# Four merge tiles moved to seven products, their sums prepared beside the second branch

## The chip, the cores and the metric

The kernel runs on one core of a Trainium2 chip. Its engines are named as in the profile: PE (TensorE, the matrix engine; PEld are its weight loads), DVE (VectorE), ACT (ScalarE), POOL (GpSimd), and SP (SyncE), which here only issues DMAs. Each engine works through its own instructions in order. The metric is the device time of one launch in microseconds.

## The reference

One layer of an encoder with three parallel branches, for a prompt of 512 rows and a sample of 256 rows, each with 16 meta rows in front. The model width is 2048, everything is fp32.

```
h = rmsnorm(z, norm_g)
cols = h @ w_in                     # to u_a, gate_a, q, k, v, gate_b, glr, x_c, gate_c, merge
y_a = s5_mixer(u_a, ...)  * silu(gate_a)      # state space model; GLU at its end: z * sigmoid(z @ w_glu + b)
y_b = gla_mixer(q, k, v, glr, ...) * silu(gate_b)   # gated linear attention, chunks of 64
y_c = rglru_mixer(x_c, ...) * silu(gate_c)    # convolution and gated linear recurrence
gates = sigmoid(merge).reshape(b, l, 3, 2048)
m = gates_0 * (y_a @ w_out_a) + gates_1 * (y_b @ w_out_b) + gates_2 * (y_c @ w_out_c)
out = rmsnorm(z + m @ w_o)          # the meta rows are dropped
```

The part of `w_in` that matters here is `merge`: 3 x 2048 columns, in the kernel 48 tiles of 128 columns.

## The kernel before

Everything is kept transposed: 128 model columns on the partitions, the rows of both sequences beside one another as 784 columns (16 meta, 512 prompt, 256 sample). The normalised x is held on chip in 16 tiles of 128, each split in two halves `xh` and `xl` (`split`: a ScalarE copy to fp32r and a VectorE subtraction), and written to memory as `xnorm`. An fp32 product is three matmuls: high by high, high by low, low by high.

A tile of `w_in` of 128 columns is projected in one of two ways. The first is the plain one: 16 k tiles x 3 x 2 halves of 384 columns = 96 matmuls (`proj`, L199, or `fill_step`, L273, one k at a time: a step is 6 matmuls). A tile takes two weight loads of 512 KB, each split in halves `hi` and `lo`. The second is Strassen's (`strassen`, `products`, L1149): two tiles together, with the 16 k tiles in two halves and the 768 columns in two halves, need seven products in place of eight, each over 8 k tiles, in four quarters `sb` of 42 matmuls: 168 for two tiles in place of 192. It needs sums of x: three of 384 columns for each k (operands 0, 1, 2), and a fourth that overwrites the second half of x itself (`t2`). `NG2` pairs are gates and `NST` pairs are merge tiles.

The program runs the branches one after another: S5, GLA, LRU, then the Strassen stage, then the output projections. Merge tiles done the plain way are no stage of their own: their steps are put between the instructions of the branches, to keep PE at work while it would wait. How many is set by a count of VectorE's work: `tick` emits a step for each 1/rate us of it, with the rate of the stage from `FILLS` (`pace`). In S5 the stages are the scan, the chunk_out steps (L652 to L655, eight of them, one after another through a round trip `kt` to `kd` to `tp` in memory on ScalarE's queue) and the end: the gelu of y (tiles `fu`, `fy`, `ft`, giving z0 to z3 as `fz`, with halves `fh` and `fl`) and then the GLU with `w_glu` (`fw`, L728, 96 matmuls). `flush` ends an open tile, and what is left of the merge tiles stands at the end of LRU as `cover`, beside which the x sums of the Strassen stage are made (`sums`, and for the overwritten part `last_sum`, after the cover). A scheduler then sets the order on each engine by its own estimate, so that the order in the code is not the one in the program.

SP issues nearly all loads in order; a load waits until its target tile is free, and what is behind it waits too.

Of the kernel before, what the change touches and what calls it, by code (L numbers as in the profile page):

```python
# [6 lines left out]
F32 = mybir.dt.float32  # L7
F32R = mybir.dt.float32r
I32 = mybir.dt.int32
AF = mybir.ActivationFunctionType  # L10
ALU = mybir.AluOpType
# [5 lines left out]
NT = NP_ + NS  # L17
# [3 lines left out]
HN = NT // 2  # L21
MAGIC = 12582912.0
FILLS = (0.2, 0.7, 1.6, 0.8, 1.1, 0, 0, 0)
# [3 lines left out]
NST = 15  # L27
# [4 lines left out]
XS = 2  # L32
# [63 lines left out]
def build(tc, A, out_p, out_s):  # L96
# [12 lines left out]
    xnorm = drm.tile([16, 128, NT], F32, name="xnorm")  # L109

# [628 lines left out]
def branch_gla(E):  # L739
    tc, A = E["tc"], E["A"]  # L740
    V, S, PE, SP = E["V"], E["S"], E["PE"], E["SP"]
    col, split, proj, evac, tick, psB = (E[k] for k in ("col", "split", "proj", "evac", "tick", "psB"))
# [11 lines left out]
    def tmp():  # L754
        return lp.tile([128, T], F32, name="tmp", bufs=4)

# [25 lines left out]
    for hp in range(2):  # L782
# [139 lines left out]
        for h in range(2):  # L922
# [22 lines left out]
            tick()  # L945
    lp.release()
# [613 lines left out]
def strassen(E):  # L1560
# [11 lines left out]
    sh, sl = [[None] * 8 for i in range(3)], [[None] * 8 for i in range(3)]  # L1572
    for k in range(8):
        for i in range(3):
            sh[i][k] = sp.tile([128, HN], F32R, name=f"sh{i}{k}")
            sl[i][k] = sp.tile([128, HN], F32R, name=f"sl{i}{k}")
    xp = tc.alloc_tile_pool(name="stx", bufs=1, reuse_waits="tile")

    def load(k, o, n, **kw):
        x = xp.tile([128, n], F32, **kw)  # L1580
        (S if k % 8 < XS else SP).dma_start(x[:], xnorm[k, :, o:o + n])
        return x[:]

    def sums(k):
        xa = load(k, 0, NT, name="xa", bufs=2)
        s_, x, u = load(k + 8, HN, HN, name="x", bufs=2), xa[:, :HN], xa[:, HN:]
        V.tensor_tensor(out=s_, in0=s_, in1=u, op=add)
        split(sh[0][k][:], sl[0][k][:], s_)
        V.tensor_tensor(out=s_, in0=s_, in1=x, op=sub)
        split(sh[1][k][:], sl[1][k][:], s_)  # L1590
        V.tensor_tensor(out=u, in0=u, in1=x, op=sub)
        split(sh[2][k][:], sl[2][k][:], u)

    def last_sum(k):

        x = load(k + 8, 0, HN, name="x", bufs=2)
        s_ = xp.tile([128, HN], F32, name="y", bufs=2)[:]
        V.tensor_tensor(out=s_, in0=sh[1][k][:].bitcast(F32), in1=sl[1][k][:].bitcast(F32), op=add)
        V.tensor_tensor(out=s_, in0=x, in1=s_, op=sub)
        split(xh[k][:, t2], xl[k][:, t2], s_)  # L1600

    n = max(1, len(merges))
    for k in range(8):
        sums(k)
        while len(merges) > max(1, n * (7 - k) // 8):
            E["cover"](16)
    E["cover"](16 * len(merges) + 16)

    xp.release()
    tp = tc.alloc_tile_pool(name="stt", bufs=1, reuse_waits="tile")  # L1610
    xp = tc.alloc_tile_pool(name="sty", bufs=2, reuse_waits="tile")
# [14 lines left out]
    def operand(a, k):  # L1626
        if isinstance(a, int):
            return sh[a][k][:], sl[a][k][:]
        tk, ts = k + 8 * (a[1] == "2"), t1 if a[0] == "1" else t2
        return xh[tk][:, ts], xl[tk][:, ts]  # L1630

    ahead = []
    for sb in range(4):
        if sb < 3:
            ahead.append(weights(0, sb))
        last_sum(2 * sb)
        last_sum(2 * sb + 1)
    xp.release()
# [28 lines left out]
    free = [f"s{p}{i}{k}" for k in range(8) for i in range(3) for p in "hl"]  # L1667
    yh, yl = [], []
    for k in range(8):
        h = E["act"].tile([128, NT], F32R, name=f"h{8 + k}")  # L1670
        l = E["act"].tile([128, NT], F32R, name=f"l{8 + k}")
        for o in (0, HN):
            yr = sp.tile([128, HN], F32, name=free.pop(0))
            SP.dma_start(yr[:], E["yspill"][k, :, o:o + HN])
            split(h[:, o:o + HN], l[:, o:o + HN], yr[:])
        yh.append(h)
        yl.append(l)
# [118 lines left out]
```

## Time and profile before

| | |
|---|---|
| time, median of 3 runs | 2037.04 us (2035.94 to 2038.36) |
| profiled execution, its own time | 2038.42 us |
| its span, first to last instruction | 2036.6 us |
| PE busy | 2003.8 us, 98% |
| DVE busy | 1504.9 us, 74% |
| ACT busy | 808.2 us, 40% |
| DMA | 252.12 MB, mean 124 GB/s |

The times of the rows below are of the profiled execution, counted from the start of its span. An instruction's length in the matmul rows overlaps with its neighbours; the distance of starts tells what one costs. In the profile S5's chunk_out steps lie at 286 to 350 us, its GLU ends at 412, the last cover begins at 766 and the first Strassen product stands behind it.

### The profile page before, as it was taken

To read this page: it belongs to the slowest core of one execution; us is meant where nothing else is said; L and a number is where in the kernel's file an instruction comes from. 1 tells how busy PE (TensorE), PEld (TensorE's weight loads), DVE (VectorE), ACT (ScalarE), POOL (GpSimd) and SP (SyncE) were. 2 spreads that over 40 slices of the span, in tenths; PEclk is the share of its full clock that TensorE was granted. 3 is DMA by queue.
4 is the path that set the end of the run, shared out by engine and by line. 5 is a ranking of instruction groups with operands and counts; after the bars stand their busy time and mean duration, and the time that the engine had idled before them with its cause. 6 is when DMAs were issued, how large, how long until landed. Compare 5 with 4: busy or idle time off the path is not lost.

```text
span 2036.6 us, 30982 instructions
## 1 busy us (share of the span) xinstructions
PE 2003.8 (98%) x12228; PEld 1972.5 (97%) x12228; DVE 1504.9 (74%) x2784; ACT 808.2 (40%) x1172; POOL 0.2 (0%) x4
## 2 busy tenths in 40 slices
PE   8999999999999999999999999999999999999997
PEld 8999999999989999999999999999999999999997
DVE  8988983656567876977676656665669989887778
ACT  7332111443437675433333222222235435533345
POOL 0000000000000000000000000000000000000000
PEclk9999999999999999999999999999999999999999
DMA  8762234421111323543443222322355335532256
GB/s 292 251 123 94 75 102 120 147 80 49 61 52 45 102 72 122 179 133 102 139 135 112 94 94 100 103 91 100 104 183 215 125 114 180 176 117 94 94 163 218
DMA packets 105378, 252.12 MB, mean 124 GB/s; under 512 B 18960, under 2 KB 39952, under 8 KB 105232
## 3 DMA queue, kind: packets, MB, share of 16 engines
q1 hardware_dynamic: 77072, 200.61, 30.8%
q10 hardware_dynamic: 28160, 49.53, 6.9%
q8 instruction: 96, 1.57, 0.3%
q14 instruction: 50, 0.41, 0.1%
HBM read 200.65 MB, written 49.45 MB: 123 GB/s over the span
## 4 chain that ended last, share of the span: by engine, by line
PE 78%; DVE 13%; ACT 4%; DMA 3%; issue 1%; ACTq 0%; SPq 0%; DVEq 0%
PE pm L1149 24%; PE br L1149 23%; PE pm L199 10%; PE pm L273 5%; PE br L1422 4%; PE pm L1292 2%; PE br L1292 2%; DVE sc L61 2%; DVE W L61 2%; PE pm L332 2%; DVE lo L61 2%; ACT gt L89 1%; DMA c<-gspill 1%; DVE hb L61 1%; PE br L199 1%
## 5 line engine op out<-in xcount | busy, mean ns | idle before, releaser
L89 ACT ACTIVATE hi<-raw 128x768 fp32r<-128x768 f32 (+2 forms) x234 | 216.1, 924 | 482.8 <-PE br L1149 129.0
L61 DVE TENSOR_TENSOR lo<-raw,hi 128x768 fp32r<-128x768 f32 (+2 forms) x234 | 246.3, 1053 | 131.5 <-ACT hi L89 131.1
L61 DVE TENSOR_TENSOR lo<-t,hi 128x1024 fp32r<-128x1024 f32 x140 | 171.5, 1225 | 193.4 <-ACT hi L89 193.2
L89 ACT ACTIVATE hi<-t 128x1024 fp32r<-128x1024 f32 x140 | 148.4, 1060 | 279.6 <-PE pm L1149 138.3
L1149 PE MATMUL pm<-l,hi 128*128 128x384 f32 (+1 forms) x616 | 197.3, 320 | 0.0
L1149 PE MATMUL pm<-h,hi 128*128 128x384 f32 (+1 forms) x616 | 196.6, 319 | 0.2 <-ACT g L89 0.2
L1149 PE MATMUL pm<-h,lo 128*128 128x384 f32 (+1 forms) x616 | 196.6, 319 | 0.0
L1149 PE MATMUL br<-l,hi 128*128 128x384 f32 (+1 forms) x504 | 167.1, 331 | 0.0
L1149 PE MATMUL br<-h,hi 128*128 128x384 f32 (+1 forms) x504 | 165.9, 329 | 0.0
L1149 PE MATMUL br<-h,lo 128*128 128x384 f32 (+1 forms) x504 | 165.8, 329 | 0.0
L199 PE MATMUL pm<-h,hi 128*128 128x392 f32 (+1 forms) x608 | 161.8, 344 | 1.2 <-ACT xp L1022 1.2
L199 PE MATMUL pm<-h,lo 128*128 128x392 f32 (+1 forms) x608 | 159.5, 342 | 1.0 <-DVE lo L61 1.0
L199 PE MATMUL pm<-l,hi 128*128 128x392 f32 (+1 forms) x608 | 159.6, 341 | 0.0
L273 PE MATMUL pm<-h,lo 128*128 128x384 f32 x512 | 131.6, 338 | 2.5 <-DVE lo L61 2.5
L273 PE MATMUL pm<-h,hi 128*128 128x384 f32 x512 | 133.8, 342 | 0.0
L273 PE MATMUL pm<-l,hi 128*128 128x384 f32 x512 | 132.6, 340 | 0.0
L1149 PEld LDWEIGHTS pm<-h,hi 128*128 128x128 f32 x616 | 115.7, 188 | 0.7 <-ACT g L89 0.5
L1149 PEld LDWEIGHTS pm<-h,lo 128*128 128x128 f32 x616 | 116.0, 188 | 0.0
L1149 PEld LDWEIGHTS pm<-l,hi 128*128 128x128 f32 x616 | 115.7, 188 | 0.0
L199 PEld LDWEIGHTS pm<-h,hi 128*128 128x128 f32 x608 | 111.0, 188 | 2.7 <-ACT xp L1022 1.5
L199 PEld LDWEIGHTS pm<-h,lo 128*128 128x128 f32 x608 | 111.2, 188 | 1.5 <-DVE lo L61 1.3
L199 PEld LDWEIGHTS pm<-l,hi 128*128 128x128 f32 x608 | 110.6, 188 | 0.2
(358 smaller groups left out, 4799.6 us busy)
## 6 DMA issues: line engine op xcount, KB each, us to landing
raw<-in_w_st SPq DMA_DIRECT2D x92, 512.0 KB
raw<-in_w_in SPq DMA_DIRECT2D x74, 512.0 KB
gspill<-g ACTq DMA_DIRECT2D x48, 384.0 KB
raw<-in_w_ost SPq DMA_DIRECT2D x32, 512.0 KB
xr<-in_xT SPq DMA_DIRECT2D x31, 392.0 KB
m<-gspill SPq DMA_DIRECT2D x26, 384.0 KB
raw<-in_w_out SPq DMA_DIRECT2D x16, 512.0 KB
raw<-in_w_outc SPq DMA_DIRECT2D x16, 512.0 KB
```

The source lines that it names most:

```text
L61: return f(*a, **k)
L89: ins = self.eng.activation(**k)
L199: PE.matmul(ps[h][:, :nw], w[:, k, :], xx[kt][:, n0 + h * nw:n0 + (h + 1) * nw], start=(kt == 0 and j == 0), stop=(kt == 15 and j == 2))
L273: PE.matmul(ps[h][:, :HN], w[:, k % 8, :], xx[k][:, NM + h * HN:NM + (h + 1) * HN], start=(k == 0 and j == 0), stop=(k == 15 and j == 2))
L332: PE.matmul(ps0[2 * t + h][:, :HT], w[:, k, :], xx[kt][:, h * HT:(h + 1) * HT], start=(kt == 0 and j == 0), stop=(kt == 15 and j == 2))
L1149: PE.matmul(ps[j][:, :nt], w[:, wi, kk, :], x, start=(k == 0 and q == 0), stop=(k == n - 1 and q == 2))
L1292: PE.matmul(ps[h][:, :HN], w[:, 4 * b + k, :], yy[4 * b + k][:, h * HN:(h + 1) * HN], start=(k == 0 and j == 0), stop=(k == 3 and j == 2))
L1422: PE.matmul(po[:, :NS], x[:, n, :], y[k][:, ss], start=(first and j == 0), stop=(last and j == 2))
```

## The change

`NST` goes from 15 to 17, so that four more merge tiles (two pairs) are done by seven products and four fewer by plain steps. The rates of two S5 stages go down, of the chunk_out stage from 0.8 to 0.15 and of the gelu stage from 1.1 to 0.85. The sums of x are made by `strassen_sums` in GLA, one k at every third `tick` of it, on VectorE and ScalarE, and their halves are written to a new memory tensor `sspill`; the Strassen stage only loads them (`fetch`, `fetch_last`). The loads of the first two sums, which stood on ScalarE's queue (`XS`), are gone. At the end of the Strassen stage `yspill` is loaded in whole tiles of 768 columns.

```diff
-FILLS = (0.2, 0.7, 1.6, 0.8, 1.1, 0, 0, 0)
+FILLS = (0.2, 0.7, 1.6, 0.15, 0.85, 0, 0, 0)
-NST = 15
+NST = 17
-XS = 2
+    sspill = drm.tile([8, 2, 2, 128, NT], F32, name="sspill")
...
 def branch_gla(E):
+    def strassen_sums(k):
+        a, b = (lp.tile([128, NT], F32, name=n) for n in ("pa", "pb"))
+        SP.dma_start(a[:], E["xnorm"][k])
+        SP.dma_start(b[:], E["xnorm"][k + 8])
+        t1, t2 = slice(0, HN), slice(HN, NT)
+        TT = lambda o, x, y, op: V.tensor_tensor(out=o, in0=x, in1=y, op=op)
+        TT(b[:, t2], b[:, t2], a[:, t2], ALU.add)
+        TT(a[:, t2], a[:, t2], a[:, t1], ALU.subtract)
+        TT(a[:, t1], b[:, t2], a[:, t1], ALU.subtract)
+        TT(b[:, t1], b[:, t1], a[:, t1], ALU.subtract)
+        for i, x in enumerate((a, b)):
+            h = lp.tile([128, NT], F32R, name="ph")
+            S.activation(out=h[:], in_=x[:], func=AF.Copy)
+            TT(x[:].bitcast(F32R), x[:], h[:].bitcast(F32), ALU.subtract)
+            SP.dma_start(E["sspill"][k, i, 0], h[:].bitcast(F32))
+            SP.dma_start(E["sspill"][k, i, 1], x[:])
+    beside = [k for k in range(8)]
+    ticks = [0]
+    def tick():
+        E["tick"]()
+        ticks[0] += 1
+        if ticks[0] % 3 == 0 and beside:
+            strassen_sums(beside.pop(0))
...
 def strassen(E):
+    s1, s23, spill = {}, {}, E["sspill"]
+    def fetch(k):
+        s1[k] = [sp.tile([128, HN], F32R, name=f"s1{p}{k}") for p in "hl"]
+        s23[k] = [sp.tile([128, 2, HN], F32R, name=f"s2{p}{k}") for p in "hl"]
+        for p in range(2):
+            SP.dma_start(s1[k][p][:].bitcast(F32), spill[k, 1, p, :, HN:])
+            SP.dma_start(s23[k][p][:].bitcast(F32), spill[k, 0, p].rearrange("q (i n) -> q i n", i=2))
+    def fetch_last(k):
+        for p, x in enumerate((xh, xl)):
+            SP.dma_start(x[k][:, t2].bitcast(F32), spill[k, 1, p, :, :HN])
     for k in range(8):
-        sums(k)
-        while len(merges) > max(1, n * (7 - k) // 8):
-            E["cover"](16)
+        fetch(k)
     E["cover"](16 * len(merges) + 16)
...
     for sb in range(4):
         if sb < 3:
             ahead.append(weights(0, sb))
-        last_sum(2 * sb)
-        last_sum(2 * sb + 1)
+        fetch_last(2 * sb)
+        fetch_last(2 * sb + 1)
...
-        for o in (0, HN):
-            yr = sp.tile([128, HN], F32, name=free.pop(0))
-            SP.dma_start(yr[:], E["yspill"][k, :, o:o + HN])
-            split(h[:, o:o + HN], l[:, o:o + HN], yr[:])
+        yr = sp.tile([128, NT], F32, name=f"s2{'hl'[k % 2]}{k // 2}")
+        SP.dma_start(yr[:], E["yspill"][k])
+        split(h[:], l[:], yr[:])
```

The functions `sums`, `last_sum` and `load` go. Most lines of the changed file move (L793 is L821 there, L1149 is L1178, L1615 is L1623).

PE at the GLU of S5, before: the L728 matmuls of z0 (`fh_3583`), of z1 (`fh_3635`) and z2 (`fh_3675`) have projection matmuls (L199) between them.

```order
L728 MATMUL br<-fh_3583,fwl 128x384
L199 MATMUL pm<-h_102,hi 128x384 x2
L199 MATMUL pm<-l_103,hi 128x384 x2
L728 MATMUL br<-fh_3635,fwh 128x384 x4
L199 MATMUL pm<-h_102,lo 128x384 x2
L199 MATMUL pm<-h_123,hi 128x384 x2
L728 MATMUL br<-fl_3636,fwh 128x384
...
L199 MATMUL pm<-l_227,hi 128x384 x2
L199 MATMUL pm<-h_226,lo 128x384 x2
L199 MATMUL pm<-h_247,hi 128x384
L728 MATMUL br<-fh_3675,fwh 128x384 x4
```

The same place in the changed program: the L728 matmuls follow one another, here the end of z1 (`fh_3486`), z2 (`fh_3520`) and the first of z3 (`fh_3566`).

```order
L728 MATMUL br<-fl_3487,fwh 128x384
L728 MATMUL br<-fh_3486,fwl 128x384
L728 MATMUL br<-fh_3520,fwh 128x384 x4
L728 MATMUL br<-fl_3521,fwh 128x384
L728 MATMUL br<-fh_3520,fwl 128x384
...
L728 MATMUL br<-fh_3566,fwh 128x384 x3
...
L728 MATMUL br<-fl_3567,fwh 128x384
L728 MATMUL br<-fh_3566,fwl 128x384
```

In the changed program 144 projection matmuls (L199) stand ahead of this run of 96 and 10 behind it, then the gate matmuls of GLA (L821). Before, 84 merge and 96 projection matmuls stood ahead, 56 between, and 51 behind.

SP at the start of the Strassen stage, before: loads of `xnorm` (`xa`, `x`) for the sums, with the weights of the products (`in_w_st`) between them.

```order
L1581 DMA xa_7714<-xnorm_70 128x768
L1581 DMA x_7716<-xnorm_70 128x384
L1581 DMA xa_7727<-xnorm_70 128x768
L1581 DMA x_7729<-xnorm_70 128x384
L1615 DMA raw_7971<-in_w_st 128x1024
L1581 DMA xa_7740<-xnorm_70 128x768
L1581 DMA x_7742<-xnorm_70 128x384
L1581 DMA xa_7753<-xnorm_70 128x768
L1581 DMA x_7755<-xnorm_70 128x384
L1615 DMA raw_7999<-in_w_st 128x1024
L1581 DMA xa_7766<-xnorm_70 128x768
```

The same place in the changed program: the first two weight loads, then ten loads over the second half of x (`h_`, `l_` with a number, L1614), and behind these the loads of the sums (`s1h`, `s2h` and so on).

```order
L1623 DMA raw<-in_w_st 128x1024 x2
L1614 DMA l_104<-sspill 128x384
L1614 DMA h_103<-sspill 128x384
L1614 DMA l_125<-sspill 128x384
L1614 DMA h_124<-sspill 128x384
L1614 DMA l_165<-sspill 128x384
...
L1614 DMA h_206<-sspill 128x384
L1614 DMA l_207<-sspill 128x384
L1608 DMA s1h_7440<-sspill 128x384
L1609 DMA s2h_7442<-sspill 128x768
L1608 DMA s1l_7441<-sspill 128x384
```

The 32 loads of sums stand there in one row; the third weight load of the products follows the last of them, then the six last loads over x. Both the ten and the six write into tiles that the last plain merge tile reads.

## Rows read from the trace of the kernel before

**Rows 1.** The page, section 1: busy us, share of the span, instructions.

```profile
PE 2003.8 (98%) x12228; PEld 1972.5 (97%) x12228; DVE 1504.9 (74%) x2784; ACT 808.2 (40%) x1172; POOL 0.2 (0%) x4
```

**Rows 2.** Waits of PE: line <- releaser: us in total, times, longest us.

```profile
PE pm L273 <- DVE lo L61: 2.5, 2, 2.0
```

**Rows 3.** Windows: us, busy us (instructions) by engine, PEclk, DMA share, GB/s.

```profile
10.00:20.00 10.00, 9.74 (x53) 9.30 (x53) 9.81 (x11) 9.91 (x13) 0.00 (x0) 1.00 1.03 409
...
382.00:412.00 30.00, 27.87 (x155) 26.51 (x154) 20.71 (x21) 13.76 (x20) 0.00 (x0) 1.00 0.42 132
...
560.00:611.00 51.00, 49.42 (x280) 45.21 (x279) 34.63 (x79) 18.06 (x32) 0.00 (x0) 1.00 0.16 52
...
269.60:273.10 3.50, 3.50 (x13) 3.50 (x12) 3.31 (x16) 0.95 (x1) 0.00 (x0) 0.51 0.41 150
...
761.10:764.60 3.50, 3.50 (x12) 3.47 (x12) 0.00 (x1) 2.38 (x4) 0.00 (x0) 0.51 0.00 0
```

**Rows 4.** Chain of waits, 300 to 432 us: start us, us, what.

```profile
304.77 4.23 PE pm L273 x24
...
328.16 14.73 PE pm L273 x84
...
350.32 14.57 PE pm L273 x83
...
367.74 7.94 DMA fy<-yd
...
379.70 3.52 DMA fy<-yd
...
412.00 8.96 PE pm L199 x51
```

**Rows 5.** Timeline of ACT beside chunk_out: start us, us, instruction.

```profile
299.93 2.47 ACTq L644 DMA_DIRECT2D tp<-kd  x4
...
307.20 2.47 ACTq L644 DMA_DIRECT2D tp<-kd  x4
```

**Rows 6.** Timeline of ACT, 350 to 415 us (in brackets: idle before).

```profile
364.92 0.87 ACT L89 ACTIVATE g<-pm 128x384 f32<-128x384 f32 x2 [14.08 <-PE pm L273]
...
383.16 0.83 ACT L89 ACTIVATE fh<-fz 128x768 fp32r<-128x768 f32 x1
...
393.08 0.84 ACT L89 ACTIVATE fh<-fz 128x768 fp32r<-128x768 f32 x1 [0.69 <-DVE fz L61]
...
396.42 0.85 ACT L89 ACTIVATE fh<-fz 128x768 fp32r<-128x768 f32 x1 [1.02 <-DVE fz L61]
```

**Rows 7.** Chain of waits, 760 to 872 us.

```profile
766.48 16.98 PE pm L273 x97
...
850.38 2.11 PE br L1149 x12
```

**Rows 8.** Timeline of PE: the first instruction behind three idles.

```profile
268.94 0.62 PE L273 MATMUL pm<-h,lo 128*128 128x384 f32 x2 [2.04 <-DVE lo L61]
...
759.90 1.01 PE L1053 MATMUL br<-xch,gwh 128*128 128x402 f32 x4 [1.92 <-ACT xch L89]
...
854.67 0.45 PE L1149 MATMUL pm<-sh,lo 128*128 128x384 f32 x1 [0.78 <-DVE lo L61]
```

**Rows 9.** Timeline of SP's DMA queue: loads of x, first and last yspill load.

```profile
12.57 8.25 SPq L159 DMA_DIRECT2D xr<-in_xT  x7
...
1493.15 0.33 SPq L1674 DMA_DIRECT2D sh<-yspill  x1
...
1502.92 0.43 SPq L1674 DMA_DIRECT2D sl<-yspill  x1
```

**Rows 10.** Groups by shape, DVE: form xcount | busy us, mean ns.

```profile
L61 DVE TENSOR_TENSOR m<-m,m 128x768 f32<-128x768 f32 x26 | 23.7, 953 | 0.0
...
L61 DVE TENSOR_TENSOR x<-x,xa 128x384 f32<-128x384 f32 x16 | 8.6, 554 | 9.1 <-DMA x<-xnorm 9.1
```

**Rows 11.** Groups by shape, ACT.

```profile
L89 ACT ACTIVATE hi<-raw 128x768 fp32r<-128x768 f32 x140 | 118.3, 845 | 267.8 <-PE br L1149 128.6 <-PE pm L1149 125.2 <-PE br L1422 6.4
```

More of the change, by code (lines that the diff above doesn't have):

```diff
@@ L741, in branch_gla @@
     V, S, PE, SP = E["V"], E["S"], E["PE"], E["SP"]
-    col, split, proj, evac, tick, psB = (E[k] for k in ("col", "split", "proj", "evac", "tick", "psB"))
+    col, split, proj, evac, psB = (E[k] for k in ("col", "split", "proj", "evac", "psB"))
     ones, ident = E["ones"], E["ident"]
@@ L945, in branch_gla @@
             tick()
+    assert not beside
     lp.release()
@@ L1571, in strassen @@
     sp = tc.alloc_tile_pool(name="st", bufs=1, reuse_waits="tile")
-    sh, sl = [[None] * 8 for i in range(3)], [[None] * 8 for i in range(3)]
-    for k in range(8):
[L1574 to L1603, printed above, removed]
-        sums(k)
-        while len(merges) > max(1, n * (7 - k) // 8):
-            E["cover"](16)
+    s1, s23, spill = {}, {}, E["sspill"]
[8 more added lines that the diff above has]
+            SP.dma_start(x[k][:, t2].bitcast(F32), spill[k, 1, p, :, :HN])
+    for k in range(8):
+        fetch(k)
     E["cover"](16 * len(merges) + 16)
-    xp.release()
     tp = tc.alloc_tile_pool(name="stt", bufs=1, reuse_waits="tile")
-    xp = tc.alloc_tile_pool(name="sty", bufs=2, reuse_waits="tile")
     def weights(i, sb):
@@ L1627, in operand @@
         if isinstance(a, int):
-            return sh[a][k][:], sl[a][k][:]
+            return (s1[k][0][:], s1[k][1][:]) if a == 0 else (s23[k][0][:, a - 1], s23[k][1][:, a - 1])
         tk, ts = k + 8 * (a[1] == "2"), t1 if a[0] == "1" else t2
@@ L1635, in strassen @@
             ahead.append(weights(0, sb))
-        last_sum(2 * sb)
-        last_sum(2 * sb + 1)
-    xp.release()
+        fetch_last(2 * sb)
+        fetch_last(2 * sb + 1)
     xp = tc.alloc_tile_pool(name="stu", bufs=1, reuse_waits="tile")
@@ L1665, in strassen @@
             S.dma_start(E["gspill"][d, :, b, :], g[:])
-    free = [f"s{p}{i}{k}" for k in range(8) for i in range(3) for p in "hl"]
     yh, yl = [], []
```

## The prediction

> **What bounds the kernel now.** I read the page first: TensorE is busy for 2003.8 of 2036.6 us [rows 1]. So any matmul that goes is worth its own length, as long as nothing takes its place, and the next question is where TensorE stands still. The view of its waits answers that: the sums are small (L273 waited 2.5 us in all, 2.0 of it at once, for a `lo` weight half [rows 2]); one wait of 1.92 us for `xch` stands beside it [rows 8]. The windows show the exception that matters: in 382 to 412 us, beside S5's gated end, PE is busy for 27.87 of 30 us; in the GLA window 560 to 611 it is 49.42 of 51 [rows 3]. Those are the stretches where work on other engines can show. Two windows at half clock (0.51) are the third thing to see; each begins right behind one of the two longest idles [rows 3, 8]. Only then did I read the chains of waits, for what the end of S5 [rows 4 to 6] and the start of the Strassen stage [rows 7] hang on.
>
> **The tensor work itself.** Four merge tiles of 96 matmuls go (L273, 384 in all) and two pairs of 168 come, so 48 matmuls less. The Strassen matmuls stand 12 in 2.11 us and the merge tiles 97 in 16.98 us [rows 7], 0.1755 us each: 48 x 0.1755 = **-8.4 us**. This is all that the change can take off TensorE's own work. Of the 384, 192 go at the end of LRU (480 to 288) and the other 192 in S5: 18 beside the scan, 90 beside the chunk_out steps (216 to 126) and 84 behind the last of these. 48 projection matmuls move forward to the place between the chunk_out steps.
>
> **The old start of Strassen.** The sums of the x operands were split beside the cover, and the weight split waited behind them on VectorE: PE idled 0.78 us at 854.67 [rows 8]. With the sums gone from there, this idle goes: **-0.8 us**.
>
> **S5's end.** Three pieces. Beside the scan PE has one wait of 2.0 us and is fed otherwise [rows 2], so the 18 return their 3.2 us. Beside chunk_out they don't all return: a step there also needs ScalarE's copy, the round trip of `kd` and four `tp` issues, 299.93 to 307.20 from one issue to the next, 7.3 us [rows 5], while 24 merge matmuls last 4.23 us [rows 4] and the step's own matmuls fill the rest. With 10 to 13 matmuls the step gets to this chain's length and no shorter. In the last long cover, 84 matmuls of 14.73 us [rows 4] give way to 47 merge and 48 projection matmuls, which are longer. I get 4.5 us from the chunk_out steps where the work removed is 90 x 0.1755 - 48 x 0.18 = 7.2: 2.7 us lost.
>
> Behind the last chunk_out step the old program has 84 merge, 203 projection and 96 gate (L728) matmuls from 350.15 to 420.95 [rows 4]: 67.6 us of work and 3.2 of idle. The projections stand between the groups of L728 there and hide the chain that makes z0 to z3. The new order has 144 projection matmuls first, and then the 96 of L728 in one run, with 10 behind. The work is 154 x 0.18 + 96 x 0.176 = 44.5 us. But z1 stands on ScalarE behind a copy of weights that waits until the end of the 144, some 26 us after the last chunk_out step (L). The issue of `fy` comes at about L+10, since ScalarE no longer sits behind a tile's end until 364.92 [rows 6]; it lands 7.94 us later, the third and fourth loads wait for buffers and land 3.52 us after issue [rows 4], and z2 and z3 come 3.3 us after each other at the quickest (393.08 to 396.42) [rows 6], about 5 with the load. That puts z3's low half at L+36 to L+38, when PE, from L+26 on, has 36 matmuls (6.3 us) that do without it. So it stalls 4 to 6 us; I take 6 with the waits between the earlier z, 3 more than the 3.2 that were there. With the 2.7 the S5 end loses **+6 us** (5.7). Bounds: if the z chain and the chunk_out chain are both covered, 0, and 3 below that if the old idle goes as well; if z3 comes as late behind z2 as z2 did behind z1 before (383.16 to 393.08 [rows 6], 9.9 us), +10.
>
> **The fetch at the start of Strassen.** Before, 6.3 MB of xnorm came in beside the cover, paced by the splits. Now 12.6 MB of ready sums come in, and SP's order puts 10 of the 192 KB loads first, which overwrite x and so wait for matmuls of the last merge tile. The 32 loads behind them wait for no such thing, but stand in the same queue. The first can go 16.3 us before the cover's end T0, since the last tile lasts 96 x 0.1755 = 16.8. The weights of the third quarter come behind all 42: 11.4 + 0.5 = 11.9 MB. PE needs them after 84 products, at T0+14.7. Seven loads of x took 8.25 us [rows 9], 401 KB each, 340 GB/s: 35.1 us, and 0.85 for ScalarE's split of 768 columns [rows 11]: T0+19.6, a stall of 4.9. Sixteen of the same small loads (yspill) took 10.2 us [rows 9], which would give 6.4; at the 409 GB/s of 10 to 20 us [rows 3] the load is there at T0+13.7 and nothing is lost. I take the nearest kind of row, x: **+5 us**, from 0 to 7.
>
> The Trainium skill ("DMA: Bandwidth & Descriptors", section "Where 436 GB/s comes from") says that a load from memory is bound near 358 GB/s per core, and the fabric at 435. The row of 409 GB/s lies above the first figure, so here the second would be the bound; by it an estimate of the 11.9 MB is 27.4 us and the stall is nil, by the first 33.3 us and 3.1. Neither enters the sum, which goes by the rows.
>
> **The clock.** Behind each idle of 2.0 and 1.9 us [rows 8] the granted clock was 0.51 for 3.5 us [rows 3], which costs 1.7 us. The stall at the fetch would be longer than these, that at S5's end comes in pieces. I put in half of one drop, **+0.9** (0 to 3.4).
>
> **The sums in GLA.** Eight times: four TensorTensor of 384 columns (0.55 us), two of 768 (0.95) [rows 10] and two ScalarE copies (0.85) [rows 11]: 33 us on VectorE and 14 on ScalarE. The same work left the Strassen start. VectorE was busy for 34.63 of 51 us at 560 to 611 [rows 3], so there is room on average; DMA share 0.16 leaves room for 25 MB spread over 200 us. What can show is one sum ahead of a latency chain of GLA: bounds 0 and 1.6 us lost in that window again in four windows, 6 us. I take **+1**, near the lower end, as PE has projections to run in most of it. The yspill reload in whole tiles moves the same bytes under running matmuls: 0.
>
> **Sum.** -8.4 - 0.8 + 5.7 + 5 + 0.9 + 1 = +3.4 on the profiled execution's 2038.4: 2041.8. That execution lies 1.4 us above the median of the runs shown, so **2040.4 us**.
>
> **Rivals.**
> Full gain: the z chain and the fetch are both covered. For it: PE is 98% busy and hides most chains; DMA ran at 409 GB/s once; S5's end was already short of cover before, so the idle there could even shrink. Against it: L728 in one run has no cover at all. Then -8.4 - 0.8 + 1 = -8.2, as a median 2028.8.
> The fetch is covered, S5's end is not: -8.4 - 0.8 + 5.7 + 1 = -2.5, 2034.5. By the 435 GB/s of the Trainium skill's "DMA: Bandwidth & Descriptors" (section "Where 436 GB/s comes from") this would be the outcome.
> Slower, by SP's queue in GLA: each of the 32 spills waits in SP's order for ScalarE or VectorE, and the weight loads of the projections stand behind them. It decides where a load comes later than the 48 matmuls (8.4 us) that the weights before it last. A late weight half in S5 cost 2.0 us and a clock drop of 1.7 [rows 2, 3, 8]; with two or three of the eight sums late, 3.7 x 2.5 = +9 on top of the forecast: 2049. Against it: GLA's DMA share is low, and SP then waits for buffers anyway.
>
> **Chances.** Forecast (2036 to 2046) 0.45: slower 0.22, same 0.20, faster 0.03. Full gain 0.27, all faster. Fetch alone covered 0.13: faster 0.05, same 0.08. SP's queue 0.15, slower. A measurement of this kernel can tell about 0.2% (4 us) from no change. That makes faster 0.35, same 0.28, slower 0.37. The range takes in the full gain, with most of the 3 us below it if S5's old idle goes too, and the SP case: 2026 to 2050; the forecast's own is 2036 to 2046.
>
> **What would show it.** L728 in one run with PE idle before z2 and z3 for 4 to 6 us in all: S5's end right. An idle of PE some 14.7 us after the first Strassen product, ended by the third weight split, with DMA share near 1 for the 30 us before it: the fetch right; none there: wrong. A window of 0.5 clock behind it settles the drop. In GLA, weights that PE waits for, with SP waiting on `pa`, `pb` or `ph`, would speak for the slower rival. The forecast is wrong if PE's busy time falls by 8 us and the span with it.

## The result and the profile after

The changed kernel is slower: 2063.12 us (median of 4 runs, 2061.01 to 2065.19) against 2036.49 (4 runs, 2035.85 to 2038.36), a ratio of 1.0127 (95% interval 1.0112 to 1.0142). That is 26.6 us (1.3%) more where 3.4 were forecast, and outside the range. The profiled execution took 2065.19 us with a span of 2063.4. Section 1 of its page, against [rows 1]:

```profile
PE 2008.0 (97%) x12180; PEld 1972.3 (96%) x12180; DVE 1522.7 (74%) x2798; ACT 808.2 (39%) x1150; POOL 0.2 (0%) x4
```

The 48 matmuls are gone, and yet PE is busy for 4.2 us more: part of them ran at half clock (granted clock 0.5, the lower of its two levels, 1.2 GHz). DMA moved 277.29 MB in place of 252.12. The waits of PE (columns as in [rows 2]):

```profile
PE br L1178 <- ACT hi L88: 8.3, 1, 8.3
...
PE br L880 <- DVE tmp L60: 4.7, 2, 2.4
PE br L728 <- ACT fh L88: 3.5, 1, 3.5
PE pm L199 <- ACT kk L88: 3.2, 1, 3.2
...
PE br L728 <- ACT fwh L88: 1.4, 1, 1.4
PE br L728 <- DVE fwl L60: 1.4, 1, 1.4
```

Those six lines are three places: the start of the Strassen stage (L1178), the chains of GLA (L880), and S5's GLU with what stands behind it. The starts of PE's instructions give the time by stretch ("gate" is the first L821 matmul of GLA, L793 before; the LRU stretch runs between its first and last L1082, L1053 before):

| stretch | before | after | difference | forecast |
|---|---|---|---|---|
| start to GLA's gate | 420.8 | 404.3 | -16.5 | -28.0 |
| gate to LRU's first matmul | 197.7 | 207.1 | +9.4 | +1 |
| LRU | 147.6 | 146.1 | -1.5 | 0 |
| rest of the cover | 76.3 | 42.7 | -33.6 | -33.7 |
| Strassen stage, first to last L1178 | 1132.8 | 1201.7 | +68.9 | +63.2 |
| output, to PE's last start | 49.4 | 49.4 | 0 | 0 |

(28.0 is the 192 matmuls of 33.7 us less 5.7; 63.2 is 336 matmuls of 59.0 us, less 0.8, plus 5; the 0.9 for the clock was put in no stretch.) LRU's -1.5 is clock as well: its last idle, 1.92 us before [rows 8] and 1.91 now at 752.78, had 3.5 us of 0.51 behind it before [rows 3] and has 1.00 now.

**S5's GLU.** PE in the run of 96, each idle and what ended it:

```profile
373.68 0.44 PE L728 MATMUL br<-fl,fwh 128*128 128x384 f32 x1 [0.72 <-DVE fl L60]
378.89 1.50 PE L728 MATMUL br<-fh,fwh 128*128 128x384 f32 x4 [3.53 <-ACT fh L88]
386.61 0.44 PE L728 MATMUL br<-fh,fwh 128*128 128x384 f32 x1 [1.44 <-ACT fwh L88]
388.93 0.44 PE L728 MATMUL br<-fh,fwl 128*128 128x384 f32 x1 [1.36 <-DVE fwl L60]
401.58 0.83 PE L199 MATMUL pm<-h,hi 128*128 128x392 f32 x2 [3.16 <-ACT kk L88]
```

The windows over it and over the other places (columns as in [rows 3]):

```profile
378.90:382.40 3.50, 3.43 (x10) 2.83 (x11) 2.55 (x4) 1.69 (x2) 0.00 (x0) 0.53 0.28 83
386.00:392.00 6.00, 4.03 (x15) 3.72 (x16) 3.57 (x4) 1.19 (x3) 0.00 (x0) 0.78 0.34 131
401.50:404.30 2.80, 2.71 (x11) 2.52 (x12) 1.29 (x4) 1.19 (x4) 0.00 (x0) 0.76 0.49 194
404.30:408.00 3.70, 3.70 (x10) 2.06 (x9) 2.85 (x6) 1.72 (x3) 0.00 (x0) 0.72 0.00 0
449.00:452.00 3.00, 3.00 (x16) 2.32 (x17) 2.44 (x7) 1.48 (x3) 0.00 (x0) 1.00 0.38 148
546.00:553.00 7.00, 6.89 (x20) 5.21 (x21) 4.90 (x13) 1.57 (x3) 0.00 (x0) 0.52 0.14 56
783.00:823.00 40.00, 32.02 (x184) 31.70 (x182) 14.56 (x21) 5.95 (x9) 0.00 (x0) 0.96 0.98 355
784.29:822.30 38.01, 30.73 (x176) 30.41 (x175) 12.66 (x17) 4.88 (x8) 0.00 (x0) 0.96 1.01 367
800.00:815.00 15.00, 15.00 (x87) 14.70 (x85) 2.18 (x2) 2.67 (x4) 0.00 (x0) 1.00 1.04 387
823.00:829.50 6.50, 6.22 (x19) 5.86 (x20) 5.21 (x9) 2.12 (x3) 0.00 (x0) 0.50 0.66 240
```

The z chain is as forecast (0.7 and 3.5 us). Three things are not: the second half of the GLU's weights (`fwh`, `fwl`, two buffers each) is ready only when the run wants it; at the run's end the next projection waits 3.16 us until `kk` has left its PSUM tile, where 51 projections stood before [rows 4]; and the clock falls behind three of these idles.

**Start of the Strassen stage.** SP's queue, PE at the third quarter, and the chain between them:

```profile
784.29 0.33 SPq L1614 DMA_DIRECT2D l<-sspill  x1
...
815.57 0.33 SPq L1623 DMA_DIRECT2D raw<-in_w_st  x1
```

```profile
823.27 0.69 PE L1178 MATMUL br<-h,hi 128*128 128x384 f32 x1 [8.26 <-ACT hi L88]
```

```profile
809.50 6.00 DMA s1h<-sspill
815.50 0.02 issue
815.52 0.03 SPq L1623
815.54 0.03 issue
815.57 6.72 DMA raw<-in_w_st
```

The first product starts at 800.2 (T0), the first load 15.9 us ahead of it; the third weights are issued at T0+15.4, land at T0+22.1 and are split at T0+23. The DMA engines are full for all of it: 1.01 of the 38.0 us from the first load to the landing, at 367 GB/s. By queue, in this window (packets, MB, share; q1 is SP's, q10 ScalarE's):

```profile
q1 hardware_dynamic: 6498, 12.36, 89.8%
q10 hardware_dynamic: 569, 1.55, 10.6%
```

The loads up to the third weights are 11.93 MB. The other 2.0 MB are four spills of 384 KB that ScalarE issued (`hspill`, `gspill`) and 0.4 MB of loads that stand behind the weights. Behind the stall the clock is at 0.50 for 6.5 us, 3.3 us more.

**GLA.** VectorE in front of the first late `tmp`:

```profile
445.79 0.56 DVE L60 TENSOR_TENSOR pb<-pb,pa 128x384 f32<-128x384 f32 x1 [7.69 <-DMA pb<-xnorm]
446.26 1.22 DVE L60 TENSOR_TENSOR lo<-raw,hi 128x1024 fp32r<-128x1024 f32 x1
447.40 0.55 DVE L60 TENSOR_TENSOR pa<-pa 128x384 f32<-128x384 f32 x1
447.87 1.83 DVE L60 TENSOR_TENSOR tmp<-tmp,kk 128x784 f32<-128x784 f32 x2
```

VectorE stands for 7.69 us at a sum whose `pb` is not there. There is one buffer for it, and SP issues the load only when the spill of the sum before has landed:

```profile
436.31 0.32 SPq L774 DMA_DIRECT2D sspill<-pb  x1
...
442.62 0.32 SPq L762 DMA_DIRECT2D pb<-xnorm  x1
```

Behind it in its order stand the weight half and the `tmp` (tile `kd`) that PE's transposes (L880) wait for. The same comes again at 544.52. PE's two idles there are 4.7 us, the clock of 0.52 from 546 to 553 costs 3.4 (7.0 x 0.48) and the 0.72 right behind the gate 1.0: together 9.1 of the 9.4 of the table. The 1.0 belongs to S5's last idle and not to the sums. In the kernel before PE stands still in this stretch once, 1.16 us at 610.53, and so it does now at 603.43.

### The profile page after: what moved, and what is told of

The parts are those of the page before. It is cut to its first block, busy times and chain, and to the rows that moved or that the text cites. A ratio compares the mean times of both kernels' runs of the same rounds, so it can differ in the third digit from the quotient of the medians.

```text
span 2063.4 us, 31021 instructions
## 1 busy us (share of the span) xinstructions
PE 2008.0 (97%) x12180; PEld 1972.3 (96%) x12180; DVE 1522.7 (74%) x2798; ACT 808.2 (39%) x1150; POOL 0.2 (0%) x4
## 2 busy tenths in 40 slices
DMA packets 114594, 277.29 MB, mean 134 GB/s; under 512 B 19984, under 2 KB 40976, under 8 KB 114448
## 4 chain that ended last, share of the span: by engine, by line
PE 57%; DMA 2%; DVE 1%; ACT 0%; SPq 0%; issue 0%; DVEq 0%; ACTq 0%
PE br L1178 25%; PE pm L1178 23%; PE pm L1451 4%; PE br L1321 2%; PE pm L1321 2%; DMA c<-gspill 1%; PE br L1451 1%; DMA s1h<-sspill 1%; DVE c L60 0%; DVE m L60 0%; DMA raw<-in_w_st 0%; DMA s2h<-sspill 0%; DVE lo L60 0%; DMA hspill<-hb 0%; DMA m<-yspill 0%; ACT c L88 0%
## 5 line engine op out<-in xcount | busy, mean ns | idle before, releaser
L1178 PE MATMUL br<-h,hi 128*128 128x384 f32 (+1 forms) x656 | 210.9, 321 | 8.3 <-ACT hi L88 8.3
L1178 PE MATMUL br<-l,hi 128*128 128x384 f32 (+1 forms) x656 | 211.6, 323 | 0.0
L1178 PE MATMUL br<-h,lo 128*128 128x384 f32 (+1 forms) x656 | 211.0, 322 | 0.0
L1178 PE MATMUL pm<-l,hi 128*128 128x384 f32 (+1 forms) x528 | 175.6, 332 | 0.1
L1178 PE MATMUL pm<-h,hi 128*128 128x384 f32 (+1 forms) x528 | 174.3, 330 | 0.0
L1178 PE MATMUL pm<-h,lo 128*128 128x384 f32 (+1 forms) x528 | 174.3, 330 | 0.0
L199 PE MATMUL pm<-h,hi 128*128 128x392 f32 (+1 forms) x608 | 161.8, 345 | 4.3 <-ACT kk L88 3.2
L199 PE MATMUL pm<-h,lo 128*128 128x392 f32 (+1 forms) x608 | 160.7, 344 | 1.0 <-DVE lo L60 1.0
L199 PE MATMUL pm<-l,hi 128*128 128x392 f32 (+1 forms) x608 | 160.5, 343 | 0.0
L1178 PEld LDWEIGHTS br<-h,hi 128*128 128x128 f32 x656 | 123.7, 189 | 8.8 <-ACT hi L88 8.6
L1178 PEld LDWEIGHTS br<-h,lo 128*128 128x128 f32 x656 | 124.1, 189 | 0.4 <-DVE lo L60 0.4
L1178 PEld LDWEIGHTS br<-l,hi 128*128 128x128 f32 x656 | 123.7, 189 | 0.0
L60 DVE TENSOR_TENSOR t<-raw 128x512 f32<-128x512 f32 x148 | 101.6, 687 | 22.8 <-DMA raw<-in_w_st 16.7
L199 PEld LDWEIGHTS pm<-h,hi 128*128 128x128 f32 x608 | 111.4, 188 | 6.2 <-ACT kk L88 3.7
L199 PEld LDWEIGHTS pm<-h,lo 128*128 128x128 f32 x608 | 111.4, 189 | 1.8 <-DVE lo L60 1.3
L199 PEld LDWEIGHTS pm<-l,hi 128*128 128x128 f32 x608 | 111.5, 189 | 0.2
```

The costliest lines, as they stand in the source:

```text
L60: return f(*a, **k)
L199: PE.matmul(ps[h][:, :nw], w[:, k, :], xx[kt][:, n0 + h * nw:n0 + (h + 1) * nw], start=(kt == 0 and j == 0), stop=(kt == 15 and j == 2))
L1178: PE.matmul(ps[j][:, :nt], w[:, wi, kk, :], x, start=(k == 0 and q == 0), stop=(k == n - 1 and q == 2))
```

## The experiments

Times are medians of rounds against runs of the kernel before on the same chip (2037.8 to 2038.2); "as the changed kernel" means that only the edit shown differs from it.

**1. The fill rates alone**, in the kernel before:

```diff
-FILLS = (0.2, 0.7, 1.6, 0.8, 1.1, 0, 0, 0)
+FILLS = (0.2, 0.7, 1.6, 0.15, 0.85, 0, 0, 0)
```

> The kernel before with the new FILLS alone: 192 merge matmuls (33.7 us) leave S5 and stand at the end of LRU instead (672 in place of 480); nothing is done in GLA and nothing is fetched. Theory of three places (the loss lies in S5's end, in GLA and at the Strassen start, each for itself): S5 gives back only the 16.5 us that the changed kernel showed between the first gate matmul of before (420.8) and its own (404.3), so the time rises by 33.7 - 16.5 = 17 us, to about 2053.5. Rival, the sum as it was predicted (S5 loses 5.7 us and what is beyond it comes from the sums and their traffic): about 2042. A rise of under 8 us speaks for the rival.

2053.45 us, ratio 1.008 (1.0065 to 1.0095). The gate comes at 402.9, 17.9 us earlier for 33.7 us of work that left S5. So the S5 part costs some 16 us by itself, as the theory had it, with the idles of the changed kernel at the same instructions:

```profile
378.02 1.65 PE L728 MATMUL br<-fh,fwh 128*128 128x384 f32 x4 [3.53 <-ACT fh L89]
386.85 0.44 PE L728 MATMUL br<-fh,fwh 128*128 128x384 f32 x1 [1.26 <-ACT fwh L89]
389.17 0.44 PE L728 MATMUL br<-fh,fwl 128*128 128x384 f32 x1 [1.36 <-DVE fwl L61]
400.24 0.83 PE L199 MATMUL pm<-h,hi 128*128 128x392 f32 x2 [3.17 <-ACT kk L89]
```

From the gate to LRU it takes 198.9 us, 1.2 more than before, though there is no sum in it.

**2. One rate back** (as the changed kernel; one tile more in S5, a cover of 192):

```diff
-FILLS = (0.2, 0.7, 1.6, 0.15, 0.85, 0, 0, 0)
+FILLS = (0.2, 0.7, 1.6, 0.15, 1.1, 0, 0, 0)
```

> The changed kernel with the gelu rate back at 1.1 (chunk_out rate stays 0.15): one merge tile (96 matmuls, 16.9 us) returns to S5, the GLU's matmuls have projection matmuls between them again, and LRU's cover falls from 288 to 192 matmuls. Theory: S5's end lost its time in the run of 96 GLU matmuls without cover (idles of 11 us and half clock behind them), so the tile goes into idle time: the first gate matmul comes at 404 + 5 or less instead of 421, and the time falls by 10 to 13 us, to 2050 to 2053. Rival: the chunk_out chain on ScalarE is where S5 loses, the tile only moves, and the time stays within 3 us of 2063.

2064.08, ratio 1.0123. The gate moves by 8.8 us for 16.9 us of work: of the GLU's idles one of 1.19 us is left, so 8 us came back. But the weights of the second and third quarter now come late by 7.5 and 6.3 us. The tile helps S5 as much as the cover misses it: the theory's 2050 to 2053 missed, and the rival's time came for another reason than the rival's.

**3. Both rates back**, 17 pairs and a cover of 96:

> The changed kernel with the old FILLS: S5 as before (gate at about 421), and all 384 matmuls less come out of LRU's cover (480 to 96). Theory: S5's end loses 17 us by FILLS, as shown alone, and this comes back; the shorter cover can cost 0 to 10 us, since the fetch starts with the last merge tile and needs memory that LRU's tail on VectorE holds, which lasts 31 us from the start of the cover whatever its length: 2046 to 2056. Rival: the cover was needed as much as S5's, the time stays within 4 us of 2063.

2067.46, ratio 1.0146, beyond both expectations. S5 is as before (gate 419.8), and the Strassen stage stands still twice:

```profile
803.52 0.69 PE L1178 MATMUL br<-h,hi 128*128 128x384 f32 x1 [21.29 <-ACT hi L88]
824.16 0.69 PE L1178 MATMUL br<-h,hi 128*128 128x384 f32 x1 [6.98 <-ACT hi L88]
```

The first of the two is not a matter of bytes, for the DMA engines are at 0.30:

```profile
782.00:803.00 21.00, 0.23 (x2) 0.00 (x0) 15.29 (x21) 6.61 (x8) 0.00 (x0) 0.62 0.30 96
```

SP stands there with the loads of the sums, 9.1 us at one until a `gspill` and 10.7 at another until an `hspill` of LRU's end has landed. So the cover hides LRU's own tail too.

**4. The sums alone**, 15 pairs and the old rates:

```diff
-NST = 17
+NST = 15
```

> The changed kernel with NST 15 and the old FILLS, so that only the sums have moved: made in GLA, spilled and fetched; no matmul moves (S5 as before, cover of 480). Theory of three separate losses: 2063.1 = 2037 + 17 (FILLS alone) - 8.4 (48 matmuls) + X, so X is about 18 us, GLA 9 and the Strassen start 9: about 2054 to 2056. Rival: GLA's part came from the earlier start of GLA or the fetch's from the shorter cover, and the sums alone cost 8 us or less: 2040 to 2045.

2041.84 (9 runs), ratio 1.0022 (1.0012 to 1.0031). With a cover of 480 the loads of the sums start at 806.58, 43 us ahead of the first product; no stall, and the stage is 2.4 us shorter than before. GLA loses 9.6 us here too. So the rival's 2040 to 2045 came and not the theory's 2054 to 2056: GLA's part belongs to the sums themselves, the fetch's comes with the shorter cover. The four covers in a row: 480 matmuls no stall, 288 8.3 us, 192 13.8, 96 28.3. Length is not all that changes among them: in this run SP's order has the loads of the sums ahead of those over x, in every run with 17 pairs behind them, and with covers of 192 and 96 the second weights stand behind the sums too. The sums ahead of the loads over x in the changed kernel were not tried.

**5. Half of the loads later** (sums of k 4 to 7 behind the third weights):

```diff
-    for k in range(8):
+    for k in range(4):
         fetch(k)
...
+        if sb > 1:
+            fetch(2 * sb)
+            fetch(2 * sb + 1)
```

> The changed kernel with the loads of the sums of k 4 to 7 behind the third weight load of the products (26 loads ahead of it instead of 42). Theory: the stall of 8.3 us at 814.7 is the place of this one load in SP's queue; with 7.2 MB ahead of it and not 11.9 it lands before it is wanted, the bytes then decide only for the fourth quarter (14 MB from T0-16 at 350 GB/s: T0+24 against T0+22), 2 to 4 us are left and no or a shorter clock drop: 2063 - 6 = 2057 (2055 to 2059). Rival, bandwidth alone: the stall moves to the fourth quarter with its whole length, 2062 to 2064.

2063.6 (2060.48 to 2069.39). The wait is not gone but comes a quarter later, at 828.28, and is 6.45 us. The bytes are the same; their order moves the stall.

**6. Half of the loads left out.** The sums of k 4 to 7 are not loaded; the products read those of k-4, so that half of the sums are left out of the computation.

> The changed kernel without the fetch of the sums of k 4 to 7 (the operands of these k read the sums of k 0 to 3 instead; the rest is as it was): 4.7 MB less between the last merge tile and the third quarter of the first products. Theory (bytes): with the queue in need order the stall only moved to the fourth quarter, 6.6 us, so the DMA rate over about 13 MB sets it; with 8.4 MB in all the data is there before T0+15, no stall of over 1 us is left, no half clock, and the time falls by 9 to 11 us, to about 2053. Rival: what is late is something with a fixed time (the last merge tile, the third weight slot, the landing of one load), and the stall stays over 4 us.

In the profiled execution (2051.08 us) the stall is gone and the clock stays up; the stage takes 1192.1 us, 9.6 less:

```profile
783.00:823.00 40.00, 40.00 (x231) 40.00 (x230) 20.59 (x30) 9.93 (x12) 0.00 (x0) 1.00 0.82 289
823.00:829.50 6.50, 6.50 (x39) 6.50 (x38) 6.27 (x12) 4.13 (x5) 0.00 (x0) 1.00 0.05 6
```

The rest of what this execution is shorter by lies in stretches that the edit doesn't touch (from the gate to LRU 3 us). The four runs spread (2051.08, 2057.37, 2061.8, 2061.83; median 2059.58). The first had a mean clock of 0.995, the other three 0.992, against 0.991 in the changed kernel, so these lost some 6 us more at half clock, an estimate from the two means; where, and whether the stall was back in them, no profile shows. So one execution shows that the bytes make the stall, and the median doesn't show its size.

**7. The sums at other ticks.** The expectation under this name speaks of two buffers for `pb`. That is the next run; what ran here were the sums at ticks 2, 7, 9, 11, 13, 16, 21, 24 in place of every third, so the text quoted does not apply to it.

> The changed kernel with two buffers for pb (and one for ei, for the room): pb's load no longer waits until the spill of the pb before it has landed, and on VectorE no sum stands between the two groups of tmp instructions in GLA. Theory: VectorE stood at the head of its queue at the first subtraction of a sum, waiting for pb (7.7 and 4.4 us), and tmp for PE's transposes stood behind it; the two idles of PE of 2.6 and 2.5 us before L880 go, the stretch from first gate to first LRU matmul falls from 207 us to about 199, and the time to about 2055. Rival: the 33 us of added VectorE work lengthen the chains wherever the sums stand; the stretch stays at 205 or more and the time at 2061 to 2064.

2064.91, no gain: gate to LRU 205.4, PE's idles before L880 1.5 and 3.4. The scheduler puts a sum in front of the `tmp` all the same.

**8. Two buffers for `pb`** (and one for `ei`, for the room):

```diff
-        a, b = (lp.tile([128, NT], F32, name=n) for n in ("pa", "pb"))
+        a, b = lp.tile([128, NT], F32, name="pa"), lp.tile([128, NT], F32, name="pb", bufs=2)
```

> The changed kernel with two buffers for pb (and one for ei, for the room): the load of pb no longer waits until the spill of the pb before it has landed, and on VectorE no sum stands between the two groups of tmp instructions in GLA. Theory: VectorE stood at the head of its queue at the first subtraction of a sum, waiting for pb (7.7 and 4.4 us at 445.8 and 544.5), and the tmp that PE's transposes need stood behind it; the idles of PE of 2.6 and 2.5 us before L880 go, the stretch from the first gate matmul to the first of LRU falls from 207 us to about 199, and the time by 6 to 9 us, to about 2056. Rival: the 33 us of added VectorE work lengthen the chains wherever the sums stand; the stretch stays at 205 or more and the time within 2 us of 2063.

2067.16, ratio 1.0144. The theory's 2056 missed: VectorE now waits for `pa`, which still has one buffer, at about the same places. PE's idles stand at L850 (3.4 and 4.0 us), and the stretch is 210.1. Two buffers for both were not tried.

```profile
439.54 0.56 DVE L60 TENSOR_TENSOR pb<-pb,pa 128x384 f32<-128x384 f32 x1 [4.32 <-DMA pa<-xnorm]
...
537.76 0.56 DVE L60 TENSOR_TENSOR pb<-pb,pa 128x384 f32<-128x384 f32 x1 [4.42 <-DMA pa<-xnorm]
```

**9. The sums held behind the chain**, in the kernel of 4. The `kd` of the second direction uses the tile `pa`, so no sum can stand in front of it:

```diff
-        a, b = (lp.tile([128, NT], F32, name=n) for n in ("pa", "pb"))
+        a, b = lp.tile([128, T], F32, name="pa")[:, :NT], lp.tile([128, NT], F32, name="pb")
...
-        if ticks[0] % 3 == 0 and beside:
+        if ticks[0] in (8, 10, 12, 14, 22, 24, 26, 28):
...
-            kd = tmp()
+            kd = lp.tile([128, T], F32, name="pa") if d else tmp()
```

> The kernel of sums_alone (NST 15, old FILLS) with the sums of GLA behind the chain: the tile pa is shared with the second tmp of the kt transposes, so that no load of a sum can go, and no sum can stand on VectorE, until that chain is over; the eight sums stand beside the chunks. Theory: GLA's loss of 9.6 us was VectorE waiting at a sum for a load (pa or pb) with tmp behind it; with the sums elsewhere the stretch from the first gate matmul to the first of LRU falls from 207 to 198 to 200 us, and the time from 2042 to 2033 to 2035, below the kernel before (2037), since the old start of Strassen's 0.8 us and the sums' tail are gone too. Rival: the chunks are chains as well, and the 33 us of work and the loads hit them there; the stretch stays over 204 and the time over 2039.

2054.41, ratio 1.008. The idles before L880 are gone, and yet it is slower: PE stands for 15.0 us at the passage to LRU, where `xp` leaves its PSUM tile, and the stretch is 212.8. ScalarE there:

```profile
621.20 0.84 ACT L88 ACTIVATE ph<-pa 128x768 fp32r<-128x768 f32 x1 [9.73 <-DVE pa L60]
624.49 0.84 ACT L88 ACTIVATE ph<-pb 128x768 fp32r<-128x768 f32 x1 [2.45 <-DMA sspill<-ph]
625.24 0.47 ACT L1051 COPY xp<-pm 128x392 f32<-128x392 f32 x1
```

The copies of `xp` stand behind the two copies of the last sum, whose tiles come late. The same fault as in GLA's chains, on another engine.

**10. The same in the changed kernel:**

> The changed kernel (NST 17, new FILLS) with the same edit in GLA. Theory: the same 7 to 9 us come off, since GLA's loss does not depend on S5 or on the cover: 2054 to 2056. Rival: the idles of GLA come from the earlier start and the denser DMA traffic, and 3 us or less come off.

2079.15, ratio 1.0208: 16 us more, as 9 against 4 (12.6), with the same wait (15.2 us). The theory missed.

**11. Early ticks**, as 9 with the sums at 7, 9, 11, 13, 15 and 21, 23, 25:

> As sums_behind_chain (15 pairs, the fill rates of before, sums tied behind the kd tile of the second direction), with the sums at ticks 7, 9, 11, 13, 15 and 21, 23, 25 in place of 8, 10, 12, 14 and 22, 24, 26, 28, so that the last one ends before GLA's last output and not behind it. Theory (GLA's loss is a matter of place alone: either a sum stands in front of the tmp of a chain, or its tile holds the memory that LRU's first tile wants): the wait of 15 us at GLA's end goes or shrinks to under 4, the idles before L880 stay away, gate to first LRU gate 198 to 202 us instead of 212.8, time 2034 to 2041. Rival (the 33 us of VectorE work cost what they cost wherever they stand, since the chains of GLA hang on VectorE): the stretch stays over 206 and the time over 2045. A third way: the fifth sum now stands right in front of the kd tile of the second half (pa), so a new idle of 4 to 8 us appears about 540 us and the time is 2040 to 2046.

2042.2 (9 runs), ratio 1.0023 (1.0013 to 1.0033): 12 us better than 9, and no better than 4. The wait for `xp` is 2.21 us (1.16 before), that for `xch` at LRU's first gate matmul 2.85; the stretch is 202.4. A new idle of 1.7 us at 516 stands in front of a gate matmul (L821): VectorE waits for the third sum's `ph`, with the `tmp` that this matmul waits for behind it.

**12. Seven sums**, as 9 at ticks 8, 10, 12, 14 and 21, 23, 25; the eighth sum is left out of the computation and the seventh loaded in its place:

> As sums_behind_chain, but only seven of the eight sums are made, at ticks 8, 10, 12, 14 and 21, 23, 25; the stage loads the seventh again in place of the eighth, which is so left out of the computation. No sum stands before the second kd tile and the last one ends early. If place alone decides, both waits of GLA are away: gate to first LRU gate 197 to 200 us, time 2032 to 2036, thus at or below the time before. If the amount of VectorE work decides, 7/8 of the loss stays: over 2045.

2042.48, ratio 1.0022 (1.0013 to 1.0032). From 400 to 600 us, this kernel and then the one before:

```profile
400.00:600.00 200.00, 197.91 (x1108) 185.01 (x1108) 143.83 (x283) 84.68 (x154) 0.00 (x0) 1.00 0.39 132
```

```profile
400.00:600.00 200.00, 197.84 (x1106) 184.59 (x1105) 124.19 (x248) 77.08 (x144) 0.00 (x0) 1.00 0.17 58
```

VectorE does 19.6 us more and PE loses nothing. So in these 200 us it is place and not amount that costs. The 3.2 us that are still lost (200.9 against 197.7) lie at the passage to LRU: SP issues the load of LRU's gate weights `gw` at 611.92, behind the spills of the last sum, in place of 605.93, and PE waits 2.8 us at its first gate matmul for `xch`. Which of the two, that load or VectorE's later end, sets it is open, and both this run and 11 missed the 2032 to 2036 that place alone would have given. LRU's stretch is longer too, 150.4 against 147.6, with two pieces of half clock of 3.4 us in place of one.

**13. The early ticks in the changed kernel:**

> The changed kernel whole (17 pairs, its own fill rates) with its sums tied behind kd and at the early ticks 7, 9, 11, 13, 15, 21, 23, 25. Theory: GLA's 9.4 us come back all or for the most part, 5 to 9 us less than the changed kernel's 2063: 2054 to 2058. Rival (as with changed_behind_chain, the wait at GLA's end takes its place): 2065 or more.

2066.22, ratio 1.0137. PE's idles before L880 are gone, but at the passage to LRU it waits 3.1 us for `xp` and 2.7 for `xch`, with half clock from 597.2 to 604.0: the rival came, and the theory's 2054 to 2058 missed. The stretch fell by 2.7 us to 204.4. That is no more than it differs among kernels with the same sums in GLA (202.3 in run 3, 204.1 in run 6, 208.3 in run 2), and S5 is 0.5 us longer here, LRU 1.3 and the Strassen stage 1.6 (the stall at the third weights is 8.77).

**14 to 16. Four buffers for the GLU's weights:** in 1, in 9 and in 11.

```diff
-        raw = fp.tile([128, 4, 128], F32, name="fw")
+        raw = fp.tile([128, 4, 128], F32, name="fw", bufs=4)
```

(and the same for `fwh` and `fwl`)

> The kernel of fills_alone (before with the new FILLS) with four buffers for the GLU's weights (fw, fwh, fwl) instead of two, so that all four are loaded and split ahead of the run of 96 matmuls. Theory: of S5's loss, the two idles behind the sixth and the twelfth group (1.4 and 1.5 us, and half clock behind them) are the weights of the second half, which wait for the sigmoids of the first; they go, and the time falls by 3 to 5 us from 2053.5 to about 2049, while the 3.7 us idle for z2 and the 3.3 us at the run's end stay. Rival: the chain to z3 or the evacuation at the end is late anyway and takes up what is won; under 1.5 us.

2050.57, 2.9 us less than 1. The waits for `fwh` and `fwl` are gone; z2 then waits 4.60 us, and the 3.16 at the end stay.

> The kernel of sums_behind_chain with four buffers for the GLU's weights. Theory: in the kernel before one wait of 1.2 us for fwl stands in the GLU (404.1); it goes, 1 to 1.5 us below sums_behind_chain. Rival: the projection matmuls between the groups had hidden the chain; the new order of the groups loses as much; within 1 us.

2051.84, 2.6 us less than 9, more than the 1 to 1.5 of the theory. The gate comes 5.5 us earlier, and GLA and LRU take 4.5 more.

> The same with four buffers for the GLU's weights fw, fwh and fwl. These took 2.9 and 2.6 us off in fills_fw4 and behind_chain_fw4. Theory: 2 to 3 us less than chain_then_sums_early. Rival (with the old fill rates and projections between the L728 groups this is a matter of chance): within 1 us.

2041.81 (11 runs), 0.4 us less than 11, as the rival had it, although its gate comes 3.6 us earlier; GLA and LRU take 3.0 more. None of the versions beats the kernel before.

## Why the prediction was wrong

**The tensor work: right.** 48 matmuls fewer; the cover is 33.6 us shorter, and the Strassen stage longer by the 59.0 us of its own matmuls and what follows below. **The old idle of 0.78: right**, it is gone.

**S5's end: mechanism right, size wrong**, 17.2 us (33.7 less 16.5) where 5.7 were forecast. Beside the scan the 18 matmuls returned their 3.2 (3.1 measured). The chunk_out steps returned 2.4 us of 7.2, not 4.5; PE stood still for 2.8 us there, where before it didn't. The term that failed is "it stalls 4 to 6 us; I take 6", of 6.2 in all behind the last chunk_out step. It is 15.3 (59.8 us from there to the gate, less 44.5 of work): 4.3 for the z chain as forecast, 2.8 for weight halves, 3.2 for the PSUM tile behind the run, and some 4 us at half clock; 1 us is not placed. I asked only for the chain that was known to be long. A run of 96 matmuls with nothing between them takes the cover from each of its inputs and from what is behind it; run 2 shows it from the other side, 8 us back for one tile. By the prices given, the old work behind the last chunk_out step is 68.2 us and not 67.6, the old idle so 2.6 and not 3.2, which makes the loss forecast a little over 6; it changes nothing in the argument.

**The fetch: mechanism right, size short.** 8.3 us of stall and 3.3 of clock, in place of 5. The issue came at T0-15.9 for T0-16.3, with the engines full. The term that failed is the bytes, "11.4 + 0.5 = 11.9 MB": until the third weights had landed 13.94 MB had moved. The spills on ScalarE's queue (1.55 MB) were left out, and so were the loads that stand behind the weights and share the engines with them (0.4). The rate was better than the 340 GB/s of the sum, 367. From T0-15.9 to T0+22.1 is 38.0 us; 35.1 were forecast. Run 5 shows that another order only moves the stall, the one profiled execution of run 6 that it goes with 4.7 MB less, and runs 2 to 4 that it grows as the cover shrinks, with LRU's tail as a second cause where the cover is shortest. The sum's other row was worked out wrongly: sixteen yspill loads of 197 KB in 10.2 us are 308 GB/s, and so a stall of 8.5 us and not 6.4. That it lies at the 8.3 measured would have been luck, as neither that rate nor those bytes were the ones. The two rivals by which the fetch would be hidden fell.

**The clock:** put at +0.9 and in fact some 4 us in S5, 4.4 in GLA and 3.3 behind the fetch (all three stand within the stretches); LRU gave 1.7 back. That the one at S5's end "comes in pieces" was taken as a reason against a drop; a drop stood behind the piece of 3.5 us, one behind that of 3.2, and one behind the two of 1.4.

**GLA: wrong step.** "I take +1, near the lower end, as PE has projections to run in most of it" failed: 9.4 us, 4.7 of idles and 4.4 of clock, of which 1.0 stands behind S5's last idle (run 1 has 1.2 us more here without a sum). VectorE had room on average, and still has. What costs is an instruction that waits for a load, in front of a short chain in the same in-order queue. Run 9 held the sums back and the idles before L880 went; run 12 kept seven eighths of the work and lost nothing from 400 to 600 us. No run won the whole back, though: in 9, 11, 12 and 13 a wait stands at the passage to LRU in place of the old ones. (The 25 MB "spread over 200 us" are those of the whole kernel; the sums move 18.9 in GLA.) The rival with SP's queue named +9 for this stage, and its size is right by luck: SP did stand, 49.3 us in all for `ph` from 404 to 600 us, but PE waited for no weights between the gate and 600 us; only the 3 us of run 12 at the passage to LRU may be of its kind.

The sum of the measured terms, -8.4 - 0.8 + 17.2 + 11.6 + 9.4 - 1.5 (LRU), is +27.5, against 26.8 in the spans. Not settled are those 3 us, the spread of run 6, and whether the changed kernel's stall goes if the sums are loaded ahead of the loads over x.

## What to carry to other kernels

A filler tile that looks like spare work is cover for whatever chain ends there: before it is taken away, list every input of the run behind it, and the first instruction after it, and time each. Work put "beside" a busy engine is priced by what it may wait for and what is queued behind it, on each engine that it passes, not by busy shares. Loads that are brought ahead need a start that is early enough for their bytes, and what still uses the tiles that they overwrite sets that start.

## What the runs showed of the hardware

Behind an idle of 2.3 to 3.6 us the clock was granted at half (0.53 from 378.9, 0.52 for 7 us from 546.0), and behind one of 8.3 us too (0.50 for 6.5 us); it was at half from 389.3 to 392.7 behind two idles of 1.4 us. But behind the idle of 2.44 us at 448.98 the window 449 to 452 has 1.00, and behind the idle of 1.9 us at LRU's end it was 0.51 in the kernel before and 1.00 in the changed one, so the length of the idle alone does not tell. With a long queue of 192 and 384 KB loads one core drew 387 GB/s over 15 us, 384 in old_fills_17, but 355 over 40 us with the tail of spills and small loads at its ends. A 512 KB load issued with the engines full took 6.72 us to land.
